# Last six down rows of tokens 0 to 255 with tokens on partitions, and their closing LayerNorm along the free axis

## The chip, the cores and the metric

The kernel runs on one core of a Trainium2 chip. The metric is the device time of one launch in microseconds (us), as the median of several runs. Five engines work from queues of their own: TensorE (PE in the profile; PEld is its weight load), VectorE (DVE), ScalarE (ACT), GpSimd (POOL) and SyncE (SP). SP issues most of the DMAs, in order.

## The reference

One inference step of a one-layer decoder trunk over 512 prompt tokens and 8 x 4 sample tokens, 544 in all, with model width 1024: a SwiGLU feed-forward block with post-LayerNorm, a mixing layer (RWKV-7 heads beside a short convolution) with post-LayerNorm, a second SwiGLU block with post-LayerNorm. The change touches the end of the last block alone:

```python
def layer_norm(x, g, b):
    mu = jnp.mean(xf, axis=-1, keepdims=True)
    var = jnp.mean(jnp.square(xf - mu), axis=-1, keepdims=True)
    return (xf - mu) * lax.rsqrt(var + LN_EPS) * g + b

def swiglu(x, wg, wu, wd):
    return (jax.nn.silu(x @ wg) * (x @ wu)) @ wd

x = layer_norm(ALPHA * x + 0.5 * swiglu(x, p["ffn2_wg"], p["ffn2_wu"], p["ffn2_wd"]), p["ln3_g"], p["ln3_b"])
```

The outputs are `x` for prompt and sample tokens and the states of the mixing layer.

## The kernel before

**Layout.** Activations lie with the 1024 features on partitions, as 8 tiles of 128, and the 544 tokens along the free axis. `z` (128 x 8 x 544) is the residual to which products are added. `HALF` splits the tokens: half 0 is 0 to 255, half 1 is 256 to 543 (288 tokens). `xhl` and `hhl` hold the block's input and the hidden rows, each value as a high and a low fp32r part; weights are loaded to a `raw` tile by SP and split into such a pair in an `hl` tile: ACT writes the high part (L134), DVE the low part (L135). A product is three matmuls (high x high, high x low, low x high; L150 to L152). The `raw` tiles form a ring of 5 in this block, the `hl` tiles a ring of 6, and `hb` tiles (`hlb` in the profile) another one.

**The second block, `f2`.** The 22 hidden rows (`DFF` = 22 x 128) come in the chunks of `CHUNKS`. The first four chunks have four rows and go through a scheme with fewer products (`pairs`, `downs`, L547 to L549). The last chunk has six rows, 16 to 21: `pairs(LAST)` makes them, and `down(LAST, d, h)` multiplies them by the down weights for output tile `d` (128 features) and half `h`: 6 rows x 3 matmuls with a 128x128 block of weights as the stationary operand and 256 or 288 tokens moving. L427 adds the sum to `z`, and `add_sum` (L320, L322) keeps a running sum of the tiles for the mean. `f2` is built with `late = 0`: `main` runs the eight `down`s of half 1, and `end` those of half 0.

**The end of the program.** `weave("l3a", ...)` lays the LayerNorm of half 1 (`layer_norm`, L222 to L268) over the `down`s of half 0: each step of the norm names the TensorE time it wants filled, and so much of the other generator is put behind it. Here the sums over features are matmuls by a matrix of 1/1024 (`ones`), so that the mean and the variance stand on all partitions. After this `layer_norm_end` does the same for half 0: mean matmuls (L275, L276, with three matmuls L278 whose result is not used), subtraction (L288), squares (L289), variance matmuls in plain f32 (L291), Ln and Exp for the inverse root (L292, L293), for two column blocks of 128 tokens; then multiplication (L297), scale and shift per feature (L301 on DVE, L303 on ACT), and a store for each two feature tiles (L304). Half 1 is stored at L315.

**What sets the order.** The code is recorded in program order with `weave`; a list scheduler then places each engine's instructions, within the bounds of `issue_after`. Each engine runs its list in order. A tile of a ring is written again only when its readers are done.

Of the kernel before, what the change touches and what calls it, by code (L numbers as in the profile page):

```python
# [12 lines left out]
F32 = mybir.dt.float32  # L13
F32R = mybir.dt.float32r
AF = mybir.ActivationFunctionType
OP = mybir.AluOpType
# [3 lines left out]
P = 128  # L20
D = 1024
KD = D // P
# [3 lines left out]
NSEQ = 8  # L26
TS = 4
T = TP + NSEQ * TS
B11, B21, B22, NT1, NT2, T3, T4 = range(7)
HALF = ((0, 256), (256, 544))  # L30
# [5 lines left out]
CHUNKS = ((0, 4), (4, 8), (8, 12), (12, 16), (16, 22))  # L36
LAST = len(CHUNKS) - 1
# [21 lines left out]


@with_exitstack
def body(ctx: ExitStack, tc: tile.TileContext, xT, gu1, wd1, win, wo_c, wo_0, wo_1, gu2, wd2, lora, vec, cst,
         sst, cstate, s0, y_o, wkvp_o, wkvs_o, shift_o, conv_o):
    nc = tc.nc
    PE, ACT, DVE, POOL = nc.tensor, nc.scalar, nc.vector, nc.gpsimd
    dma = nc.sync.dma_start

    def pool(st, name, side="left", **kw):
        return st.enter_context(tc.tile_pool(name=name, bufs=1, side=side, reuse_waits="tile", **kw))

    keep = pool(ctx, "keep")
    wp = pool(ctx, "wp")
# [14 lines left out]
    def col(v, i):  # L87
        return vc[:, v + i:v + i + 1]
# [4 lines left out]
    def sm():  # L93
        return ps.tile([P, 512], F32, name="sm", bufs=5)
# [105 lines left out]
    def weave(key, crit, *fill):  # L200
        bg.extend(fill)
        for need in crit:
            take(need * FILL[key])

    def drain(*fill):
        bg.extend(fill)
        take(1e9)
# [5 lines left out]
    def layer_norm(z, c0, c1, gcol, bcol, epsv, q, rs, s1, sink, table=None, hl2=None, both=False):  # L213
        n = c1 - c0
        pair = hl2 is None

        def mean_of(x, need):
            split(hl2[:, 0, :n], hl2[:, 1, :n], x)
            o = sm()
            yield need  # L220
            for i in range(2):
                PE.matmul(o[:, :n], onr, hl2[:, i, :n], start=(i == 0), stop=(i == 1))  # L222
            return o

        if pair:
            m = sm()
            PE.matmul(m[:, :n], ones, s1[:, :n], start=True, stop=False)
            PE.matmul(m[:, :n], ones, z[:, KD - 1, c0:c1], start=False, stop=True)
        else:
            m = yield from mean_of(s1[:, :n], 1300)  # L230
        yield 800 if pair else 300
        for j in range(4):
            zz = z[:, 2 * j:2 * j + 2, c0:c1]
            qq = q[:, 2 * j:2 * j + 2, :n]
            DVE.tensor_tensor(zz, zz, m[:, None, :n].to_broadcast([P, 2, n]), op=OP.subtract)
            sq = ACT.activation(qq, zz, AF.Square)
            if j == 0 and table == "ahead":
                tab = issue(sq, ACT.preload_act_table_set, "natural_log_exp_and_others")
            if pair:
                if j % 2:  # L240
                    DVE.tensor_tensor(q[:, 2 * j - 2:2 * j, :n], q[:, 2 * j - 2:2 * j, :n], qq, op=OP.add)
            elif j:
                DVE.tensor_tensor(q[:, 0:2, :n], q[:, 0:2, :n], qq, op=OP.add)
            yield 900 if pair else 1000
        if pair:
            v = sm()
            for i, j in enumerate((0, 1, 4, 5)):
                PE.matmul(v[:, :n], ones, q[:, j, :n], start=(i == 0), stop=(i == 3))
        else:
            DVE.tensor_tensor(q[:, 0, :n], q[:, 0, :n], q[:, 1, :n], op=OP.add)  # L250
            v = yield from mean_of(q[:, 0, :n], 900)
        yield 800 if pair else 600
        if table == "late":
            tab = issue(ACT.activation(warm, v[:, 0:1], AF.Copy), ACT.preload_act_table_set, "natural_log_exp_and_others")
        ln = ACT.activation(rs[:, :n], v[:, :n], AF.Ln, bias=epsv)
        if table:
            after(ln, tab)
        ACT.activation(rs[:, :n], rs[:, :n], AF.Exp, scale=-0.5)
        yield 1200 if pair else 600
        for d in range(0, KD, 2):  # L260
            zz = z[:, d:d + 2, c0:c1]
            DVE.tensor_tensor(zz, zz, rs[:, None, :n].to_broadcast([P, 2, n]), op=OP.mult)
            for e in (d, d + 1):
                x, g, b = z[:, e, c0:c1], col(gcol, e), col(bcol, e)
                if both and e > d:
                    DVE.tensor_scalar(x, x, g, b, op0=OP.mult, op1=OP.add)
                else:
                    ACT.activation(x, x, AF.Identity, scale=g, bias=b)  # L268
            sink(d, zz, c0, c1)
            yield 1600 if pair else 1700  # L270

    def layer_norm_end(z, gcol, bcol, epsv, q, rs, s1):

        m, o = sm(), sm()
        PE.matmul(m[:, :256], ones, s1[:, :256], start=True, stop=False)  # L275
        PE.matmul(m[:, :256], ones, z[:, KD - 1, 0:256], start=False, stop=True)  # L276
        for _ in range(3):
            PE.matmul(o[:, :256], ones, s1[:, :256], start=True, stop=True)  # L278
        cs = [slice(0, P), slice(P, 2 * P)]

        def two(x):
            return x[:, None, :].to_broadcast([P, 2, P])

        for c in cs:
            v = sm()
            for j in range(0, KD, 2):
                zz, qq = z[:, j:j + 2, c], q[:, j:j + 2, c]
                DVE.tensor_tensor(zz, zz, two(m[:, c]), op=OP.subtract)  # L288
                ACT.activation(qq, zz, AF.Square)  # L289
                for i in range(2):  # L290
                    PE.matmul(v[:, :P], ones, qq[:, i, :], start=(j + i == 0), stop=(j + i == KD - 1))  # L291
            ACT.activation(rs[:, c], v[:, :P], AF.Ln, bias=epsv)  # L292
            ACT.activation(rs[:, c], rs[:, c], AF.Exp, scale=-0.5)  # L293
        for n, c in enumerate(cs):
            for d in range(0, KD, 2):
                zz = z[:, d:d + 2, c]
                DVE.tensor_tensor(zz, zz, two(rs[:, c]), op=OP.mult)  # L297
                for e in (d, d + 1):
                    x, g, b = z[:, e, c], col(gcol, e), col(bcol, e)
                    if e % 2 or e == 6:  # L300
                        DVE.tensor_scalar(x, x, g, b, op0=OP.mult, op1=OP.add)  # L301
                    else:
                        ACT.activation(x, x, AF.Identity, scale=g, bias=b)  # L303
                dma(y_o[:, d:d + 2, c], zz)  # L304
        yield 0

    def to_x(spill):
        def sink(d, x, c0, c1):
# [3 lines left out]
        return sink  # L312

    def to_y(d, x, c0, c1):
        dma(y_o[:, d:d + 2, c0:c1], x)  # L315

    def add_sum(s1, z, d, c0, c1, top):
        n = c1 - c0
# [5 lines left out]
    class Ffn:  # L324
# [21 lines left out]

        def open_lnq(self):
            self.tst.close()
            return pool(self.tst, "lnq" + self.ph).tile([P, KD, 288], F32, name="lnq")

        def weights(self, key, src, n, pair=False):
            if key not in self.w:
# [313 lines left out]
        def main(self):  # L666
            self.open_tv()
            tv = self.inputs()
            self.raw, self.held, self.t = {}, [], 0
            self.todo, self.events = self.plan()  # L670
            z = self.z
            self.done, self.made = set(), set()
            for i, m in enumerate((3, 0, 1, 2) if self.nf > NEX else range(self.na)):
                if m >= self.nf:
                    yield from self.up(m, 0)
                yield from self.up(m, 1)
                next(tv)
                if i == 1 and self.nf < self.na:
                    for j, n in enumerate("gu"):
                        self.w[n, 3] = wload(self.gu[3, :, j, :])  # L680
                elif i in (1, 2):
                    self.t = (-12, -5)[i - 1]
                    self.feed()
            self.t = 0
            for _ in tv:
                pass
            for d in range(KD):
                ACT.activation(z[:, d], z[:, d], AF.Copy, scale=2.0 * ALPHA)
            for ci in range(LAST + 1):
                if ci:  # L690
                    yield from self.pairs(ci)
                if ci < LAST:
                    yield from self.downs(ci)
            for d in range(KD):
                yield from self.down(LAST, d, 1 - self.late)

        def end(self):
            return seq(*(self.down(LAST, d, self.late) for d in range(KD)))
# [773 lines left out]
    weave("l2b", ln2b, f2.first())  # L1472
    drain(f2.main())
    lnq = f2.open_lnq()
    weave("l3a", layer_norm(z, *HALF[1], V_LN3G, V_LN3B, epsf, lnq, f2.lnr, f2.s1[1], to_y, "ahead", f2.hl2), f2.end())
    drain()
    drain(layer_norm_end(z, V_LN3G, V_LN3B, epsf, lnq, f2.lnr, f2.s1[0]))
    f2.close()


# [3 lines left out]
def _constants():  # L1484
# [15 lines left out]
    return c  # L1500


_OUTS = [("y", (P, KD, T)), ("wkvp", (P, 4, 64)), ("wkvs", (P, 4, NSEQ, 64)), ("shift", (P, 14, 9)),
         ("conv", (P, 4, 2 + 2 * NSEQ))]


# [52 lines left out]
```

## Time and profile before

| | |
|---|---|
| median of 3 runs | 1095.28 us (1092.99 to 1095.94) |
| the profiled execution | 1092.91 us |
| its span in the profile | 1091.1 us |
| granted TensorE clock, mean over the span | 0.995 |
| PE / DVE / ACT / POOL busy | 1059.4 / 845.7 / 588.3 / 178.4 us |

Times in the profile run from the start of the span. A row of the timeline has its start, its duration, engine, line, operation, and output and inputs by the program's names; in brackets stands the idle time ahead of it and what ended it. A row of a group has the total busy time and the mean of one instruction in ns. Matmuls overlap, so the distance between two starts is what one costs, not its duration. In the windows each engine has its busy time in the stretch. In the chain of waits a row has its start and the time that it adds.

### The profile page before, as it was taken

To read this page: it belongs to the slowest core of one execution; us is meant where nothing else is said; L and a number is where in the kernel's file an instruction comes from. 1 tells how busy PE (TensorE), PEld (TensorE's weight loads), DVE (VectorE), ACT (ScalarE), POOL (GpSimd) and SP (SyncE) were. 2 spreads that over 40 slices of the span, in tenths; PEclk is the share of its full clock that TensorE was granted. 3 is DMA by queue.
4 is the path that set the end of the run, shared out by engine and by line. 5 is a ranking of instruction groups with operands and counts; after the bars stand their busy time and mean duration, and the time that the engine had idled before them with its cause. 6 is when DMAs were issued, how large, how long until landed. Compare 5 with 4: busy or idle time off the path is not lost.

```text
span 1091.1 us, 22869 instructions
## 1 busy us (share of the span) xinstructions
PE 1059.4 (97%) x9258; PEld 1019.9 (93%) x9258; DVE 845.7 (78%) x1576; ACT 588.3 (54%) x1095; POOL 178.4 (16%) x288
## 2 busy tenths in 40 slices
PE   9999999999999998999999999999999999999997
PEld 8999999999999987898889987999999999999996
DVE  7788988889775857775578558999889888887657
ACT  6645465554552767653435334667555555545425
POOL 0122220313100022142000200001312213121000
PEclk9999999999999999999999999999999999999999
DMA  8568594967853323252145625443857859677402
GB/s 281 135 128 190 119 221 122 184 151 154 193 135 117 97 95 88 63 117 70 41 140 183 145 79 174 120 135 79 180 153 154 196 117 212 153 159 172 122 1 82
DMA packets 99082, 148.88 MB, mean 136 GB/s; under 512 B 35233, under 2 KB 60577, under 8 KB 98977
## 3 DMA queue, kind: packets, MB, share of 16 engines
q1 hardware_dynamic: 71776, 111.25, 33.2%
q0 software_dynamic: 27200, 36.18, 22.0%
q8 instruction: 72, 1.18, 0.4%
q14 instruction: 34, 0.27, 0.1%
HBM read 128.74 MB, written 9.75 MB: 127 GB/s over the span
## 4 chain that ended last, share of the span: by engine, by line
PE 68%; DVE 9%; issue 9%; ACT 7%; DMA 6%; POOL 1%; SPq 0%; POOLq 0%; DVEq 0%; ACTq 0%
PE mm L547 7%; PE mm L150 7%; PE mm L548 7%; PE mm L549 7%; PE mm L151 7%; PE mm L152 7%; PE sm L549 5%; PE sm L548 5%; PE sm L547 5%; DMA raw<-in_gu 4%; ACT hl L134 3%; DVE hl L135 2%; PE sm L1042 1%; PE sm L150 1%; PE sm L151 1%
## 5 line engine op out<-in xcount | busy, mean ns | idle before, releaser
L135 DVE TENSOR_TENSOR hl<-raw,hl 128x1024 fp32r<-128x1024 f32 (+3 forms) x232 | 270.5, 1171 | 75.2 <-ACT hl L134 74.2
L134 ACT ACTIVATE hl<-raw 128x1024 fp32r<-128x1024 f32 (+3 forms) x232 | 231.8, 1013 | 88.8 <-DVE raw L514 40.5
L150 PE MATMUL mm<-xhl,hl 128*128 128x288 f32 (+1 forms) x736 | 219.7, 299 | 3.2 <-DVE z L1431 1.6
L151 PE MATMUL mm<-xhl,hl 128*128 128x288 f32 (+1 forms) x736 | 214.1, 291 | 0.3 <-DVE xhl L139 0.3
L152 PE MATMUL mm<-xhl,hl 128*128 128x288 f32 (+1 forms) x736 | 212.6, 289 | 0.1
L150 PEld LDWEIGHTS mm<-xhl,hl 128*128 128x128 f32 x736 | 139.1, 189 | 10.3 <-DVE z L1431 2.6
L151 PEld LDWEIGHTS mm<-xhl,hl 128*128 128x128 f32 x736 | 139.4, 189 | 2.6 <-issue 1.2
L152 PEld LDWEIGHTS mm<-xhl,hl 128*128 128x128 f32 x736 | 139.2, 189 | 1.2 <-DVE hl L135 0.5
L549 PE MATMUL sm<-xhl,hl 128*128 128x272 f32 x432 | 125.3, 290 | 0.0
L548 PE MATMUL sm<-xhl,hl 128*128 128x272 f32 x432 | 124.5, 288 | 0.0
L547 PE MATMUL sm<-xhl,hl 128*128 128x272 f32 x432 | 124.0, 287 | 0.0
L547 PE MATMUL mm<-tv,hl 128*128 128x272 f32 x288 | 83.2, 289 | 3.4 <-ACT cpb L608 3.1
L520 POOL DMA_DIRECT2D raw<-in_gu x36 | 43.4, 1206 | 256.9 <-DVE hlb L139 155.3
L549 PE MATMUL mm<-tv,hl 128*128 128x272 f32 x288 | 83.4, 290 | 0.0
L548 PE MATMUL mm<-tv,hl 128*128 128x272 f32 x288 | 83.1, 289 | 0.0
L547 PEld LDWEIGHTS sm<-xhl,hl 128*128 128x128 f32 x432 | 81.4, 188 | 0.0
L549 PEld LDWEIGHTS sm<-xhl,hl 128*128 128x128 f32 x432 | 81.3, 188 | 0.0
L548 PEld LDWEIGHTS sm<-xhl,hl 128*128 128x128 f32 x432 | 81.2, 188 | 0.0
L526 POOL DMA_DIRECT2D raw<-in_wd x32 | 39.3, 1482 | 248.8 <-DVE hlb L139 218.0
L547 PEld LDWEIGHTS mm<-tv,hl 128*128 128x128 f32 x288 | 54.3, 188 | 4.7 <-ACT cpb L608 4.7
L547 PE MATMUL mm<-hhl,hl 128*128 128x272 f32 x192 | 56.9, 302 | 0.7 <-DVE z L637 0.7
L547 PE MATMUL sm<-hhl,hl 128*128 128x272 f32 x192 | 55.9, 291 | 0.0
(393 smaller groups left out, 2784.0 us busy)
## 6 DMA issues: line engine op xcount, KB each, us to landing
raw<-in_gu SPq DMA_DIRECT2D x84, 512.0 KB, 4.7
raw<-in_gu POOLq DMA_DIRECT2D x36, 512.0 KB, 6.3
raw<-in_wd SPq DMA_DIRECT2D x32, 512.0 KB, 4.7
raw<-in_win SPq DMA_DIRECT2D x26, 512.0 KB, 3.6
raw<-in_wd POOLq DMA_DIRECT2D x32, 256.0 KB, 6.9
raw<-in_wd SPq DMA_DIRECT2D x16, 384.0 KB, 3.2
z<-cpb POOLq DMA_DIRECT2D x16, 272.0 KB, 9.7
z<-sv POOLq DMA_DIRECT2D x16, 272.0 KB, 6.5
```

The source lines that it names most:

```text
L134: ACT.activation(hl[:, 0, a:b], raw[:, a:b], AF.Copy)
L135: DVE.tensor_tensor(hl[:, 1, a:b], raw[:, a:b], hl[:, 0, a:b].bitcast(F32), op=OP.subtract)
L150: PE.matmul(out, wh, src[:, 0, k, c0:c1], start=(start and i == 0), stop=False)
L151: PE.matmul(out, wh, src[:, 1, k, c0:c1], start=False, stop=False)
L152: seen["fill"] = PE.matmul(out, wl, src[:, 0, k, c0:c1], start=False, stop=(stop and i == n - 1))
L520: POOL.dma_start(x.rearrange("p (s c) -> p s c", s=2), bass.AP(tensor=a11.tensor, offset=a11.offset, ap=[[2 * D, P], [P * 2 * D, 2], [1, 5 ...
L526: POOL.dma_start(four(x)[:, i], bass.AP(tensor=a11.tensor, offset=a11.offset, ap=[[DFF, P], [P * DFF, 2], [1, 256]]), accum_op=OP.add)
L547: PE.matmul(out, wh, src(0, i), start=(first and i == 0), stop=False, skip_group_check=True)
L548: PE.matmul(out, wh, src(1, i), start=False, stop=False, skip_group_check=True)
L549: PE.matmul(out, wl, src(0, i), start=False, stop=(i == n - 1), skip_group_check=True)
L1042: crit(PE.matmul(q[r0:r0 + m, o:o + nn], lhs, rhs, start=True, stop=True))
```

## The change

In `f2`, the `down`s of the last chunk are replaced for both halves.

- Half 1 (`down_wide`, in `main`): the down weights are read as six row tiles of 128 x 1024 (`wl`, one for each hidden row, all features) in place of eight tiles of 128 x 768 (one for each output tile, all six rows). Output tiles 0 to 3 are summed in four PSUM tiles row by row; then tiles 4 to 7 follow one after the other. The six split tiles are kept.
- Half 0 (`end_wide`, laid under half 1's norm): tokens stand on partitions, in two blocks of 128. Eight transposes (a matmul in transpose mode against an identity that is loaded, `eye`) put the residual `z` of the block into two PSUM tiles of 512 features; onto these the products are added, with the hidden rows (128 x 128 tokens) as the stationary operand and 512 columns of the weights moving (the last 512 features of the second block in two parts of 256).
- The norm of half 0 (`layer_norm_rows`): `bn_stats` on four parts of 256 features straight from PSUM, `bn_aggr` for mean and variance of each token, Ln and Exp on one column, and two `scalar_tensor_tensor` for each 512 features: (x - mean) * g, then * rs + b, with `g` and `b` loaded to all partitions (`gb`, 1 MB). The rows go to a new output `yt`, tokens on partitions, with 2 KB for each partition and store. `layer_norm_end` is gone; `add_sum` for half 0 too.

```diff
+    def layer_norm_rows(o, y, g, b, epsv, st, out):
+
+        for i in range(4):
+            DVE.bn_stats(st[:, 6 * i:6 * i + 6], o[i // 2][:, 256 * (i % 2):256 * (i % 2) + 256])
+        mean, rs = st[:, 24:25], st[:, 26:27]
+        DVE.bn_aggr(st[:, 24:26], st[:, 0:24])
+        ACT.activation(rs, st[:, 25:26], AF.Ln, bias=epsv)
+        ACT.activation(rs, rs, AF.Exp, scale=-0.5)
+        for i in range(2):
+            c = slice(512 * i, 512 * i + 512)
+            DVE.scalar_tensor_tensor(y[:, c], o[i], mean, g[:, c], op0=OP.subtract, op1=OP.mult)
+            DVE.scalar_tensor_tensor(y[:, c], y[:, c], rs, b[:, c], op0=OP.mult, op1=OP.add)
+            dma(out[:, c], y[:, c])
...
-        dma(y_o[:, d:d + 2, c0:c1], x)
+        dma(y_o[:, d:d + 2], x)
...
-            for d in range(KD):
-                yield from self.down(LAST, d, 1 - self.late)
+            if self.late:
+                for d in range(KD):
+                    yield from self.down(LAST, d, 0)
+            else:
+                yield from self.down_wide()
+
+        def down_wide(self):
...
+            def weights(m):
+                with ExitStack() as st:
+                    for e in self.held if m > 3 else ():
+                        st.enter_context(tc.issue_after(e.ins))
+                    return wload(wl[m])
+
+            self.wm = []
+
+            def done(d, o):
+                DVE.tensor_tensor(z[:, d, c0:c1], z[:, d, c0:c1], o[:, :n], op=OP.add)
+                add_sum(self.s1[1], z, d, c0, c1, KD)
+
+            def three(o, m, d, first, last):
+                hl, x = self.wm[m], self.hhl
+                for i, (v, y) in enumerate(((0, 0), (0, 1), (1, 0))):
+                    seen["fill"] = PE.matmul(o[:, :n], hl[:, v, P * d:P * d + P], x[:, y, m, c0:c1], start=(first and i == 0),
+                                             stop=(last and i == 2), skip_group_check=True)
+
+            os = [f() for f in (big, sm, big, sm)]
+            for m in range(n6):
+                self.wm.append(weights(m))
+                for d in range(4):
+                    three(os[d], m, d, m == 0, m == n6 - 1)
+                    if d % 2:
+                        yield 6 * (n / 2.4 + 3)
+            for d in range(4):
+                done(d, os[d])
+            for d in range(4, KD):
+                o = big() if d % 2 else sm()
+                for m in range(n6):
+                    three(o, m, d, m == 0, m == n6 - 1)
+                    if m % 2:
+                        yield 6 * (n / 2.4 + 3)
+                done(d, o)
+
+        def end_wide(self, gb, idt, st):
+            n6 = len(self.wm)
+            z, x = self.z, self.hhl
+            for t in range(2):
+                tok = slice(P * t, P * t + P)
+                o = [(sm if t else big)() for _ in range(2)]
+                for d in range(KD):
+                    PE.matmul(o[d // 4][:, P * (d % 4):P * (d % 4) + P], z[:, d, tok], idt, start=(d % 4 == 0), stop=False,
+                              is_transpose=True, skip_group_check=True)
+                yield 1500
+                for c, n in ((0, 512), (512, 256), (768, 256)) if t else ((0, 512), (512, 512)):
+                    q = o[c // 512][:, c % 512:c % 512 + n]
+                    for m in range(n6):
+                        for i, (v, y) in enumerate(((0, 0), (0, 1), (1, 0))):
+                            seen["fill"] = PE.matmul(q, x[:, y, m, tok], self.wm[m][:, v, c:c + n], start=False,
+                                                     stop=(m == n6 - 1 and i == 2), skip_group_check=True)
+                        if m % 2 or n == 512:
+                            yield 3 * n / 2.4 * (1 if n == 512 else 2)
+                layer_norm_rows(o, self.rows[t].rearrange("p a t -> p (a t)")[:, 0:D], gb[:, 0], gb[:, 1], epsf, st[:, t],
+                                yt_o[:, t])
...
-    weave("l3a", layer_norm(z, *HALF[1], V_LN3G, V_LN3B, epsf, lnq, f2.lnr, f2.s1[1], to_y, "ahead", f2.hl2), f2.end())
+    gb = f2.lp.tile([P, 2, D], F32, name="gb")
+    idt = f2.lp.tile([P, P], F32, name="idt")
+    st = f2.lp.tile([P, 2, 28], F32, name="st")
+    dma(idt, eye)
+    dma(gb, bass.AP(tensor=ln3.tensor, offset=ln3.offset, ap=[[0, P], [D, 2], [1, D]]))
+    weave("l3a", layer_norm(z, *HALF[1], V_LN3G, V_LN3B, epsf, lnq, f2.lnr, f2.s1[1], to_y, "ahead", f2.hl2),
+          f2.end_wide(gb, idt, st))
     drain()
-    drain(layer_norm_end(z, V_LN3G, V_LN3B, epsf, lnq, f2.lnr, f2.s1[0]))
     f2.close()
```

The line numbers of the changed kernel differ. In it L696 is the addition to `z` in half 1, L702 a matmul of `down_wide`, L729 a transpose, L736 a matmul of `end_wide`, L275 to L283 the instructions of `layer_norm_rows`; `layer_norm`'s own lines up to L268 have kept their numbers. On TensorE's list, the end of the program before: the last three products, then the statistics of half 0.

```order
L150 MATMUL sm<-hhl,hlb 128x256
L151 MATMUL sm<-hhl,hlb 128x256
L152 MATMUL sm<-hhl,hlb 128x256
L275 MATMUL sm<-cpb,ones 128x256
L278 MATMUL sm<-cpb,ones 128x256
L276 MATMUL sm<-z,ones 128x256
L278 MATMUL sm<-cpb,ones 128x256 x2
L291 MATMUL sm<-lnq,ones 128x128 x16
```

And now, from the last product of half 1 on (the four L222 are the mean and the variance of half 1's norm):

```order
L702 MATMUL mm<-hhl,hl 128x288 x18
L729 MATMUL mm<-idt,z 128x128 x8
L736 MATMUL mm<-hl,hhl 128x512 x3
L222 MATMUL sm<-hhl,ones 128x288
L736 MATMUL mm<-hl,hhl 128x512
L222 MATMUL sm<-hhl,ones 128x288
L736 MATMUL mm<-hl,hhl 128x512 x32
L222 MATMUL sm<-hhl,ones 128x288
L729 MATMUL sm<-idt,z 128x128 x2
L222 MATMUL sm<-hhl,ones 128x288
L729 MATMUL sm<-idt,z 128x128 x6
L736 MATMUL sm<-hl,hhl 128x512 x18
```

Behind these stand 36 more L736 with 256 columns, and nothing after them: the matmuls of half 0's norm are gone, and half 1's variance (the third L222) stands behind all products of the first token block.

VectorE's list at the end, before (L427 and L322 are the addition to `z` and the running sum, L288 to L301 half 0's norm):

```order
L427 TENSOR_TENSOR z<-z,mm 128x256
L322 TENSOR_TENSOR cpb<-cpb,z 128x256
L427 TENSOR_TENSOR z<-z,sm 128x256
L288 TENSOR_TENSOR z<-z,sm 128x2x128 x8
L297 TENSOR_TENSOR z<-z,cpb 128x2x128 x2
L301 TENSOR_SCALAR z<-z,vc 128x128 x2
L297 TENSOR_TENSOR z<-z,cpb 128x2x128 x2
L301 TENSOR_SCALAR z<-z,vc 128x128 x3
```

And now, from half 1's sums of squares (L243, L250) on; `st<-mm` and `hk` belong to the first token block, `st<-sm` and `sv` to the second, and L262 is half 1's multiplication by the inverse root:

```order
L243 TENSOR_TENSOR lnq<-lnq 128x576 x2
L250 TENSOR_TENSOR lnq<-lnq 128x288
L139 TENSOR_TENSOR hhl<-lnq,hhl 128x288
L275 BN_STATS st<-mm 128x6 x2
L277 BN_AGGR st<-st 128x2
L282 SCALAR_TENSOR_TENSOR hk<-mm,st,gb 128x512 x2
L283 SCALAR_TENSOR_TENSOR hk<-hk,st,gb 128x512 x2
L262 TENSOR_TENSOR z<-z,cpb 128x2x288 x4
L275 BN_STATS st<-sm 128x6 x4
L277 BN_AGGR st<-st 128x2
L282 SCALAR_TENSOR_TENSOR sv<-sm,st,gb 128x512 x2
L283 SCALAR_TENSOR_TENSOR sv<-sv,st,gb 128x512 x2
```

The first block's whole norm has moved ahead of half 1's L262; behind the last matmuls only the second block's is left. On SP's list the loads of `eye` and `gb` follow the last weights, and the stores of the first block stand ahead of half 1's four.

More of the change, by code (lines that the diff above doesn't have):

```diff
@@ L61, in body @@
 @with_exitstack
-def body(ctx: ExitStack, tc: tile.TileContext, xT, gu1, wd1, win, wo_c, wo_0, wo_1, gu2, wd2, lora, vec, cst,
-         sst, cstate, s0, y_o, wkvp_o, wkvs_o, shift_o, conv_o):
+def body(ctx: ExitStack, tc: tile.TileContext, xT, gu1, wd1, win, wo_c, wo_0, wo_1, gu2, wd2, wl, ln3, eye, lora, vec, cst,
+         sst, cstate, s0, y_o, yt_o, wkvp_o, wkvs_o, shift_o, conv_o):
     nc = tc.nc
@@ L270, in layer_norm @@
             yield 1600 if pair else 1700
[L272 to L305, printed above, removed]
+    def layer_norm_rows(o, y, g, b, epsv, st, out):
[10 more added lines that the diff above has]
+            dma(out[:, c], y[:, c])
     def to_x(spill):
@@ L348, in open_lnq @@
             self.tst.close()
-            return pool(self.tst, "lnq" + self.ph).tile([P, KD, 288], F32, name="lnq")
+            self.lp = pool(self.tst, "lnq" + self.ph)
+            return self.lp.tile([P, KD, 288], F32, name="lnq")
         def weights(self, key, src, n, pair=False):
@@ L693, in main @@
                     yield from self.downs(ci)
-            for d in range(KD):
-                yield from self.down(LAST, d, 1 - self.late)
+            if self.late:
[4 more added lines that the diff above has]
+        def down_wide(self):
+            m0, m1 = CHUNKS[LAST]
+            n6 = m1 - m0
+            c0, c1 = HALF[1]
+            n = c1 - c0
+            z = self.z
+            def weights(m):
[28 more added lines that the diff above has]
+                done(d, o)
@@ L1500, in _constants @@
     return c
-_OUTS = [("y", (P, KD, T)), ("wkvp", (P, 4, 64)), ("wkvs", (P, 4, NSEQ, 64)), ("shift", (P, 14, 9)),
+_OUTS = [("y", (P, KD, 288)), ("yt", (P, 2, D)), ("wkvp", (P, 4, 64)), ("wkvs", (P, 4, NSEQ, 64)), ("shift", (P, 14, 9)),
          ("conv", (P, 4, 2 + 2 * NSEQ))]
@@ L1529 @@
         a[name] = wo[:, :, k0:k1].reshape(KD // n, n, P, (k1 - k0) * P).transpose(0, 2, 1, 3).reshape(KD // n, P, D)
+    a["wl"] = g["ffn2_wd"][0][CHUNKS[LAST][0] * P:].reshape(-1, P, D)
+    a["ln3"] = np.stack([g["ln3_g"][0], g["ln3_b"][0]])
+    a["eye"] = np.eye(P, dtype=np.float32)
     a["lora"] = np.stack([np.concatenate([g["w_lora_up"][0], g["a_lora_up"][0]], 0), g["g_lora_up"][0]], 1)
@@ L1549 @@
     r = _run(nc, [arrays], core_ids=[0]).results[0]
-    y, wp, ws, sh, cv = (r["out_" + n] for n, _ in _OUTS)
-    y = y.transpose(2, 1, 0).reshape(T, D)
+    y, yt, wp, ws, sh, cv = (r["out_" + n] for n, _ in _OUTS)
+    y = np.concatenate([yt.transpose(1, 0, 2).reshape(2 * P, D), y.transpose(2, 1, 0).reshape(288, D)], 0)
     sh = sh.transpose(2, 1, 0).reshape(9, 14 * P)
```

## The prediction, made before the changed kernel ran

> **What bounds the kernel now.** I read the page first: the totals, then the chain that ended last.
>
> ```profile
> span 1091.1 us, 22869 instructions
> ...
> PE 1059.4 (97%) x9258; PEld 1019.9 (93%) x9258; DVE 845.7 (78%) x1576; ACT 588.3 (54%) x1095; POOL 178.4 (16%) x288
> ...
> PE 68%; DVE 9%; issue 9%; ACT 7%; DMA 6%; POOL 1%; SPq 0%; POOLq 0%; DVEq 0%; ACTq 0%
> ```
>
> TensorE sets the pace, so over most of the program only fewer or cheaper matmuls help. The instruction orders of the two programs are the same up to the last feed-forward chunk, so I cut the trace into the windows that the change touches: the last matmuls of half 0 (tokens 0 to 255), the closing LayerNorm, and what follows the last computation.
>
> ```profile
> core 0: us, PE busy (x) PEld busy (x) DVE busy (x) ACT busy (x) POOL busy (x), PEclk, DMA share, GB/s
> 1059.50:1077.40 17.90, 17.90 (x150) 17.56 (x149) 14.41 (x29) 9.90 (x17) 0.00 (x0) 1.00 0.14 48
> 1077.40:1088.20 10.80, 6.40 (x44) 5.47 (x42) 8.50 (x27) 6.44 (x18) 0.00 (x0) 0.92 0.33 97
> 1088.20:1091.10 2.90, 0.00 (x0) 0.00 (x0) 0.00 (x0) 0.00 (x0) 0.00 (x0) 0.50 0.42 117
> ```
>
> In the first window TensorE never rests. In the second it is idle for a third, and its 44 records belong to the norm alone. The chain of waits over that stretch shows engines handing over to one another:
>
> ```profile
> 1077.43 0.12 PE sm L152
> 1077.55 0.43 PE sm L275 x2
> 1077.98 0.43 PE sm L278 x2
> 1078.42 0.45 PE sm L276 x2
> ...
> 1079.81 2.06 PE sm L291 x16
> ...
> 1081.96 0.37 ACT cpb L292
> 1082.33 0.30 ACT lnq L289
> ...
> 1082.86 0.76 DVE z L297 x2
> ...
> 1087.94 0.26 DVE z L301
> ```
>
> From 1077.55 to 1082.86 statistics are made: 1.3 us for the mean, 1.0 for the first subtraction and square, 2.1 for the variance matmuls, 0.9 for Ln and Exp. From there to 1088.20 VectorE scales and shifts. The last matmul of the real work is 13.5 us ahead of the end of the span: this tail is what the change rewrites.
>
> **The matmuls.** Before, half 0 takes 144 matmuls of 256 columns (8 output tiles, 6 row tiles, 3 terms).
>
> ```profile
> 1059.35 0.28 PE L150 MATMUL mm<-hhl,hl 128*128 128x256 f32 x1
> ...
> 1073.11 0.28 PE L150 MATMUL mm<-hhl,hlb 128*128 128x256 f32 x1
> ...
> 1077.03 0.28 PE L150 MATMUL sm<-hhl,hlb 128*128 128x256 f32 x1
> ...
> 1077.27 0.28 PE L152 MATMUL sm<-hhl,hlb 128*128 128x256 f32 x1
> ...
> 537.56 1.02 PE L1207 MATMUL sm<-ux,BS 128*128 128x512 f32 x2
> ...
> L1207 PE MATMUL sm<-ux,BS x8: 590/592/697, 537.6 to 662.5; 128*128 128x512 f32 x8
> ...
> 433.28 0.52 PE L951 MATMUL sm<-cs,bkb 64*128 64x64 f32 x10
> ...
> L951 PE MATMUL sm<-cs,bkb 64*128 64x64 f32 x64 | 4.2, 236 | 1.4 <-ACT BK L956 1.0 <-DVE SC L940 0.3
> ```
>
> Between the second and third row lie 33 matmuls: 3.92/33 = 0.1188 us each, 17.1 for 144. From 1059.35 to 1077.39 are 18.0, so the four ones-matmuls (L222) of half 1's norm take 0.9 with their waits; they stay. The new code has 54 matmuls of 512 columns and 36 of 256. No fp32r matmul of 512 columns is in the trace. Twice the 256 row is 0.238. The plain f32 matmul of L1207 has 512 columns in two records, 1.02 less one record of 0.59, 0.43, apart, and plain f32 passes of 256 columns (L275, above) are 0.43/2 = 0.215 apart, 1.81 times the fp32r row, which puts 512 at 0.43/1.81 = 0.238 too; half of 0.43, with no overhead per instruction, is 0.215. I take 0.226, between them: 54 x 0.226 + 36 x 0.1188 = 16.5 us, 0.6 less than before; 15.9 and 17.1 at the ends.
>
> The residual now needs 16 transposes of 128x128 f32. The nearest row is L951, f32 transposes of 64x64 (236 ns busy), ten in 0.52 us: (0.52 - 0.24)/9 = 0.03 us apart, though there two row halves of the array alternate. The other side is a 128-column plain f32 matmul, two records of L291, 2.06/16 x 2 = 0.26. A transpose is one record in the trace, not two, but each loads its own 128 columns of weights, as each 256-column matmul does in 0.119. I take 0.12: 1.9 us, with 0.5 and 4.1 at the ends.
>
> The Trainium skill, "TensorE: Matmul & The Clock Gate", Part 4 (PE-mode transpose), speaks against this: it gives about 275 ns for a 128x128 bf16 transpose inside a kernel, mostly latency. If that were the spacing, 16 would take an estimated 4.4 us, and the sum below would lose 2.5 us. The L951 rows speak for a duration: 236 ns busy but 0.03 apart.
>
> TensorE then issues its last matmul's end at 1059.35 + 1.9 + 16.5 + 1.0 (L222 and 0.1 more of waiting, since fewer matmuls stand ahead of the first one) = 1078.75.
>
> **What leaves the critical path.** Mean and variance matmuls, squares, the eight subtractions and the scale and shift per column (L275 to L304) are gone; so are eight z additions and six running sums of half 0 on VectorE. For tokens 0 to 127 the new norm runs under the matmuls of tokens 128 to 255; only the second half's tail is exposed.
>
> ```profile
> 1077.59 0.42 DVE L427 TENSOR_TENSOR z<-z,sm 128x256 f32<-128x256 f32 x1 [1.26 <-PE sm L152]
> ...
> L288 DVE TENSOR_TENSOR z<-z,sm 128x256 f32<-128x256 f32 x8 | 2.7, 416 | 0.9 <-PE sm L276 0.9
> ...
> L1256 DVE SCALAR_TENSOR_TENSOR zc<-cu,vc,zc 128x512 f32<-128x512 f32 x8 | 6.0, 746 | 0.7 <-ACT zc L1254 0.7
> L1003 DVE TENSOR_TENSOR tm<-AT,De 128x15 f32<-128x15 f32 x4 | 0.7, 172 | 0.1
> L713 ACT ACTIVATE warm<-eps 128x1 f32<-128x1 f32 x1 | 0.2, 203 | 0.0
> out_y<-z SPq DMA_DIRECT2D x4, 288.0 KB, 2.3
> out_y<-z SPq DMA_DIRECT2D x8, 128.0 KB, 1.9
> ```
>
> VectorE starts 0.32 after a last matmul's start (1077.27 to 1077.59), so at 1078.63 + 0.32 = 1078.95. No bn_stats is in the trace; as a one-pass read of 256 PSUM columns it is nearest to L288, 0.42 (0.17 if it cost as little as the smallest row, 0.84 if it made two passes). Only the fourth is exposed: the others wait for column blocks done 4.3 and 2.1 us earlier. bn_aggr on 24 numbers: 0.17, from L1003. So statistics end at 1079.54. Ln and Exp on one column are 0.2 each (L713), to 1080.0, hidden by the first two scalar_tensor_tensor, which need only the mean. Four of those on 512 columns: 0.746 each, about 0.67 apart when chained (other chained VectorE rows overlap by 0.08: eight L288 of 0.416 in 2.74), 2.76 in all, to 1082.3 (0.3 less by a two-operand row, 0.2 more unchained). Then a store: before, from 1088.20 to 1091.10 are 2.9 with 128 KB; the stores are now 256 KB, and the 288 KB row lands 0.4 later: 3.3 (up to 0.5 more, as two follow each other). End of span: 1085.6.
>
> **What is hidden, and by what.** The half-1 sums are now made row tile by row tile, over four output tiles at once.
>
> ```profile
> 1040.41 0.29 PE L549 MATMUL sm<-xhl,hl 128*128 128x272 f32 x1
> ...
> 1042.72 0.73 DVE L139 TENSOR_TENSOR hhl<-sv,hhl 128x544 fp32r<-128x544 f32 x1
> ...
> 1065.47 0.76 DVE L243 TENSOR_TENSOR lnq<-lnq 128x576 f32<-128x576 f32 x1
> ...
> 1071.70 0.76 DVE L262 TENSOR_TENSOR z<-z,cpb 128x576 f32<-128x576 f32 x1
> 1072.50 4.26 ACT L268 ACTIVATE z<-z,vc 128x288 f32<-128x288 f32 x8 [0.83 <-DVE z L262]
> ...
> L135 DVE TENSOR_TENSOR hl<-raw,hl 128x1024 fp32r<-128x1024 f32 (+3 forms) x232 | 270.5, 1171 | 75.2 <-ACT hl L134 74.2
> ...
> 1040.00:1050.00 10.00, 10.00 (x76) 9.85 (x75) 7.92 (x16) 1.86 (x3) 0.00 (x0) 1.00 0.00 0
> ```
>
> A weight tile is used up in 12 matmuls, 1.6 us, where an output tile lasted 18. The first four tiles' weights are split before the last pair product is issued, by 1040.54. From there 140 matmuls fill the time to 1059.35, 0.134 each; row tile 4 is 44 of them, 5.9 us, away, at 1046.4, while its rows were ready at 1043.45 before, and the two weight splits left, now 1.17 instead of 0.95 each, end near 1045. Cover is over 1 us; without it a late split costs up to 1.2. The 64 KB identity and the 1 MB of scale and shift go out on SP's queue behind the last weights, where the 1040 to 1050 window shows no DMA traffic; neither is needed before 1059 and 1069. SP then waits for the first rows' result before half 1's stores; those follow ACT's L268 anyway.
>
> VectorE works in order: the first row block's statistics (its columns are ready at 1059.35 + 1.0 + 0.5 + 18 x 0.226 = 1064.9 and 18 matmuls later, 1069.0) stand between half 1's sums of squares (1065.47 before) and its L262. Ahead of L262 now stand two bn_stats, bn_aggr and four 512-column operations, 3.7 us, from 1069.1: L262 starts near 1073 rather than 1071.70, and ACT's L268 (4.3 us) ends near 1078, before ACT's next Ln at 1079.5. So this delay stays off the path by 1.5 us.
>
> **The sum.** The span falls from 1091.1 to 1085.6, by 5.5 us. With the 1.8 us that lie around the span the profiled execution, 1092.91, becomes 1087.4. That execution was below all three timed runs; against their median of 1095.28 the prediction is **1089.8**. The unknown prices that help add up to 1.4 + 0.6 + 0.25 + 0.3 + 0.4 (if the stores cost no more) = 3.0, those that hurt to 2.2 + 0.6 + 0.4 + 0.2 + 0.5 = 3.9: gains of 1.6 to 8.5, 1086.8 to 1093.7 for this case.
>
> **Rivals.**
> *Dear transposes.* At 0.26 each, with bn_stats in two passes, the gain is 5.5 - 2.2 - 0.4 = 2.9: 1092.4. For it: no 128x128 transpose is in the trace, and a change between f32 and fp32r may cost TensorE something that no row shows apart. Against: one record per transpose.
> *512-column matmuls at half rate.* If fp32r with 512 moving columns ran like L1207's records, 0.43 apart, 54 x (0.43 - 0.226) = 11.0 us would be added and TensorE, never idle there, would pass it all on: 1100.8, slower. It decides from 0.226 + 5.5/54 = 0.33 us. For it: L1207 is the only 512-column row. Against: its operands are plain f32, whose 256-column records also cost almost twice.
> *VectorE's and ACT's order becomes the bound.* If the first row block's norm came 5 us late, L268 would end at 1083 and hold ACT's last Ln and Exp behind it to 1083.4; the third scalar_tensor_tensor needs them at 1079.54 + 1.34 = 1080.9. The end is 2.5 later, 1092.3. For it: VectorE's queue is in order and 14.41 of 17.9 busy already. Against: it loses fourteen operations of 0.34 there and gains twelve, four of them twice as long.
> That the tail does not shrink at all would need the end to be set elsewhere; half 1's stores, last issued near 1078, land by 1081.
>
> **How the numbers follow.** Forecast 0.70; dear transposes 0.13; half rate 0.10; the order 0.07. What this kernel's measurement can tell from no change is about 0.3%, 3.3 us. The forecast's own range is beyond that for 0.67 of its 0.70; dear transposes straddle it (0.04 faster, 0.09 within), the order too (0.02 and 0.05), half rate is slower. Faster 0.73, within 0.3% 0.17, slower 0.10. The timed runs before scatter by 3 us, so I widen the case's range by 1.5 us on either side, to 1085.3 and 1095.2, which also holds the two middle rivals; half rate stays out.
>
> **What would show it.** After the change: last L736 near 1078.6; 512-column rows 0.22 to 0.24 apart; eight transposes in about 1 us; one bn_stats, bn_aggr and four scalar_tensor_tensor between the last matmul and the last store, 3.7 us; no TensorE gap after 1040 longer than 0.3 us; ACT done with L268 before the last bn_aggr. The prediction is wrong if TensorE's end moves past 1081, if the tail from last matmul to end exceeds 9 us, or if the half-1 rows show TensorE waiting for a weight split.

## The result and the profile after

| | before | after |
|---|---|---|
| median, 6 runs each | 1095.12 us (1092.99 to 1096.86) | 1089.48 us (1087.87 to 1091.27) |
| ratio | | 0.9951 (0.9936 to 0.9966) |
| the profiled execution: span | 1091.12 us | 1088.24 us |
| start of the last six down rows | 1036.75 | 1038.78 |
| from there to the end of the span | 54.37 us | 49.47 us |
| of it: half 1 | 22.60 | 22.38 |
| half 0, first instruction to the end of the last matmul | 18.20 | 19.89 |
| behind the last matmul | 13.57 | 7.20 |

The changed kernel is faster by 0.49% (0.34 to 0.64), 5.6 us between the medians. The two profiled spans lie only 2.9 apart, since this execution came 2.0 us later to the place where the programs part. Ahead of it TensorE and GpSimd have the same instructions; on ACT and VectorE only four splits of down weights differ, which are 1024 columns wide in place of 768, and SP loads those wider tiles. They are not what makes this start late: some 700 us ahead of them, at TensorE's 2500th matmul, the changed kernel is already 2.3 us behind (328.25 against 325.96). The first experiment shows how far the start scatters. What is compared below is the stretch from the first matmul of the last six down rows to the end. The ends of the spans are taken from the trace in full; the page of the profile gives them to 0.1 us, and the expectations below, worked out from it, have 54.35 and 49.42 for 54.37 and 49.47.

The chain of waits of the changed kernel over that end (start, time that the row adds, engine, line); L702 is half 1, L729 the transposes, L736 half 0's products:

```profile
1058.92 2.40 PE mm L702 x18
1061.32 0.87 PE mm L729 x8
1062.20 0.69 PE mm L736 x3
1062.89 0.36 PE sm L222
1063.24 0.23 PE mm L736
1063.48 0.26 PE sm L222
1063.73 7.43 PE mm L736 x32
1071.16 0.31 PE sm L222
1071.47 0.22 PE sm L729 x2
1071.69 0.28 PE sm L222
1071.96 0.65 PE sm L729 x6
1072.62 8.45 PE sm L736 x54
1081.06 0.02 issue
1081.08 0.77 DVE st L275 x2
...
1081.88 0.27 DVE st L277
...
1082.18 0.81 DVE sv L282 x2
```

Up to 1081.06 TensorE alone carries the chain. Behind the last product the chain before changed engines five times and took 10.6 us to the last computation; now VectorE alone stands there, for 3.8 us, and then come the stores. The timeline shows first the weight load of half 1's first mean matmul, then both norms of half 0 on VectorE and ACT (start, busy time, in brackets the idle time ahead and what ended it):

```profile
1062.84 0.19 PEld L222 LDWEIGHTS sm<-hhl,ones 128*128 128x128 f32 x1 [0.38 <-ACT hhl L138]
...
1072.51 1.42 DVE L282 SCALAR_TENSOR_TENSOR hk<-mm,st,gb 128x512 f32<-128x512 f32 x2
...
1073.84 1.41 DVE L283 SCALAR_TENSOR_TENSOR hk<-hk,st,gb 128x512 f32<-128x512 f32 x2
...
1075.16 2.76 DVE L262 TENSOR_TENSOR z<-z,cpb 128x576 f32<-128x576 f32 x4
1075.95 4.27 ACT L268 ACTIVATE z<-z,vc 128x288 f32<-128x288 f32 x8 [2.55 <-DVE z L262]
...
1077.84 0.76 DVE L275 BATCH_NORM_STATS2 st<-sm 128x6 f32<-128x256 f32 x2
1081.08 0.76 DVE L275 BATCH_NORM_STATS2 st<-sm 128x6 f32<-128x256 f32 x2 [2.49 <-PE sm L736]
1081.88 0.26 DVE L277 BATCH_NORM_AGGREGATE st<-st 128x2 f32<-128x24 f32 x1
1082.18 0.29 ACT L278 ACTIVATE st<-st,eps 128x1 f32<-128x1 f32 x1 [1.96 <-DVE st L277]
1082.18 1.41 DVE L282 SCALAR_TENSOR_TENSOR sv<-sm,st,gb 128x512 f32<-128x512 f32 x2
1082.50 0.20 ACT L279 ACTIVATE st<-st 128x1 f32<-128x1 f32 x1
1083.50 1.40 DVE L283 SCALAR_TENSOR_TENSOR sv<-sv,st,gb 128x512 f32<-128x512 f32 x2
```

The first block's norm (`hk`) runs while TensorE makes the second block's products. Of the second block's four bn_stats two start at 1077.84, and two, not one, wait 2.49 us for TensorE's last matmul. Ln and Exp end at 1082.70 beside the first two operations of 512 columns. VectorE ends at 1084.90; the last 3.3 us hold the two stores, which land 2.0 us after their issue, and the 1.3 us from there to the end of the program.

### The profile page after: what moved, and what is told of

It reads as the page before. It is cut to its first block, busy times and chain, and to the rows that moved or that the text cites. A ratio compares the mean times of both kernels' runs of the same rounds, so it can differ in the third digit from the quotient of the medians.

```text
span 1088.2 us, 22658 instructions
## 1 busy us (share of the span) xinstructions
PE 1054.5 (97%) x9178; PEld 1013.2 (93%) x9178; DVE 841.3 (77%) x1550; ACT 583.1 (54%) x1077; POOL 179.5 (16%) x288
## 4 chain that ended last, share of the span: by engine, by line
PE 69%; DVE 9%; issue 8%; ACT 6%; DMA 5%; POOL 1%; SPq 0%; DVEq 0%; POOLq 0%; ACTq 0%
PE mm L527 8%; PE mm L528 7%; PE mm L529 7%; PE mm L150 7%; PE mm L151 6%; PE mm L152 6%; PE sm L529 5%; PE sm L527 5%; PE sm L528 5%; DMA z<-cpb 2%; ACT hl L134 2%; DVE hl L135 2%; DMA raw<-in_gu 1%; PE sm L1088 1%; PE mm L702 1%
```

## The experiments

All compare the stretch defined above. Its parts are read from the timeline: the first matmul of the last six down rows, the first instruction of half 0, the end of the last product's matmul, the end of the span.

| kernel | start | end | stretch | half 1 | half 0 | behind it | time of its own run or runs |
|---|---|---|---|---|---|---|---|
| before | 1036.75 | 1091.12 | 54.37 | 22.60 | 18.20 | 13.57 | 1095.12 |
| e0_before | 1037.33 | 1091.70 | 54.37 | 22.60 | 18.20 | 13.57 | 1093.47 |
| after | 1038.78 | 1088.24 | 49.47 | 22.38 | 19.89 | 7.20 | 1089.48 |
| e1_wide_only | 1038.24 | 1092.52 | 54.27 | 22.39 | 18.19 | 13.69 | 1094.28 |
| e2_no_residual | 1035.93 | 1083.37 | 47.44 | 22.39 | 17.86 | 7.20 | 1085.14 |
| e3_norms_last | 1036.28 | 1090.40 | 54.12 | 22.39 | 20.14 | 11.59 | 1092.16 |
| e4_256 | 1042.66 | 1092.42 | 49.76 | 22.38 | 20.18 | 7.19 | 1094.18 |
| e5_third_tile | 1040.64 | 1089.99 | 49.34 | 22.39 | 19.90 | 7.05 | 1091.78 |
| e6_mean_later | 1040.34 | 1089.41 | 49.08 | 22.39 | 19.48 | 7.21 | 1091.17 |
| e7_both | 1037.76 | 1086.70 | 48.94 | 22.39 | 19.48 | 7.07 | 1087.53 |

Where a kernel ran once, its time says little: it moves with the start, by nearly 7 us between kernels that are the same up to there, while the stretch of one and the same kernel came out as 54.37 twice. Times of different jobs do not compare either: the kernel before has a median of 1095.12 in the first job and of 1092.49 (11 runs) in the one that ran e4 to e7.

**The kernel before once more** (`e0_before`, no edit).

> The kernel before, unchanged, profiled once more. The quantity that these experiments compare is the stretch from the first matmul of the last six down rows to the end of the span: 54.35 us before (1036.75 to 1091.1), 49.42 after the change (1038.78 to 1088.2). Theory (the 2.0 us by which the changed kernel reaches this stretch later is scatter of the 1037 us ahead of it, which hold the same instructions in the same order): the stretch is again 54.2 to 54.5, and the place where it starts may move by 1 to 2 us. Rival (the change itself delays what runs ahead, by where its inputs lie): the start is again 1036.5 to 1037.0 here, and near 1038.8 in every kernel with the new inputs.

The stretch is 54.37. The start moved by 0.6 here; with the new inputs it lies at 1035.93 and 1036.28 (e2, e3) as well as at 1038.78 and 1042.66. The rival falls: its 1038.8 does not recur, and the spread has no side. Why these starts scatter was not tried. The granted clock may have a part in it: the two latest starts, e4 and e5, have the lowest means over the span, 0.991 and 0.992. It is not all, since e3 starts early with 0.993 and the kernel after late with 0.995.

**The row tiles alone** (`e1_wide_only`): half 1 as in the change, half 0 from the same tiles with features on partitions, then the old norm.

```diff
-    weave("l3a", layer_norm(...), f2.end_wide(gb, idt, st))
+    weave("l3a", layer_norm(...), f2.end_rows())
     drain()
+    drain(layer_norm_end(z, V_LN3G, V_LN3B, epsf, lnq, f2.lnr, f2.s1[0]))
...
+        def end_rows(self):
+            for d in range(KD):
...
+                    for i, (v, y) in enumerate(((0, 0), (0, 1), (1, 0))):
+                        PE.matmul(o[:, :n], self.wm[m][:, v, P * d:P * d + P], self.hhl[:, y, m, c0:c1], ...)
```

> Half 1 by down_wide with the six row tiles of weights as in the change; half 0 from the same tiles but with features on partitions, 144 matmuls of 256 columns, and the old norm at the end. Theory (the row tiles cost nothing and gain nothing, all of the gain is in half 0's products and tail): stretch 54.0 to 54.6. Rival (the row tiles themselves save or cost, since TensorE no longer waits for weights or now does): stretch off 54.35 by more than 0.5.

The stretch is 54.27. Half 1 is 0.2 shorter, here as in every kernel with row tiles, and the rest is as before within 0.1; its chain has the old statistics again (L289 to L307 are the lines of the old norm here):

```profile
1076.68 2.14 PE mm L785 x18
1078.82 0.43 PE sm L289 x2
...
1081.08 2.07 PE sm L305 x16
...
1084.13 0.76 DVE z L311 x2
...
1089.21 0.26 DVE z L315
```

So nearly all of the gain comes with half 0's part of the change, its products and norm together. The row tiles, which those products read, cost nothing. They save 0.2, which the kernel before spends at 1042.74: there a weight load waits for ACT's split of the last two hidden rows (L138, 1042.03 to 1042.69), which the order by row tiles needs later.

**Without the transposes** (`e2_no_residual`).

```diff
-                for d in range(KD):
-                    PE.matmul(o[d // 4][...], z[:, d, tok], idt, start=(d % 4 == 0), stop=False, is_transpose=True, ...)
-                yield 1500
...
-   PE.matmul(q, x[:, y, m, tok], self.wm[m][:, v, c:c + n], start=False, ...)
+   PE.matmul(q, x[:, y, m, tok], self.wm[m][:, v, c:c + n], start=(m == 0 and i == 0 and c % 512 == 0), ...)
```

> The change without the 16 transposes: half 0's outputs leave out the residual. Theory (transposes are on TensorE's path at about 0.11 us each, and fewer instructions ahead of half 1's mean make it wait up to 0.5 more): stretch 1.2 to 1.8 shorter than 49.42, so 47.6 to 48.2. Rival (a transpose is latency, hidden under the next matmuls, or the change of mode costs more than the rows show): less than 0.8, or more than 2.3.

The stretch is 47.44, 2.03 shorter, all of it in half 0: a little more than expected. The transposes are on TensorE's path at their full distance, 1.74 us by the chain above (0.87 for eight, twice). Leaving them out saves some 0.3 us more, because the scheduler then finds another order: between the two L222 of a pair stand two and three products, in place of one product and two transposes, and the four L222 cost 0.86 in all, where they cost 1.21 after the change. That they would wait longer was wrong.

```profile
1060.11 0.28 PE sm L222
...
1060.85 0.13 PE sm L222
...
1068.17 0.32 PE sm L222
...
1069.20 0.13 PE sm L222
```

Neither rival holds.

**Both norms behind the last matmul** (`e3_norms_last`): the second block's first, then the first block's.

```diff
-                layer_norm_rows(o, self.rows[t]...)
+                os.append(o)
...
+            last = rows(1)
+            with tc.issue_after(last.ins):
+                rows(0)
```

> The change with the first token block's norm put behind the second's on VectorE, so that both stand behind the last matmul. Theory (the tail is VectorE's work behind the last matmul plus one store, so what is hidden now comes out in full: four bn_stats, bn_aggr and four operations of 512 columns, 1.4 + 0.3 + 2.7): stretch 4.2 to 4.6 longer than 49.42, 53.6 to 54.0, and the gain is nearly gone. Rival (the gain is in the cheaper norm, not in hiding half of it; the two blocks' work overlaps with the store): 1 to 2.5 longer.

The stretch is 54.12, 4.65 longer, 0.1 above the range, and 4.39 of it lie behind the last matmul; the rest is in half 0's matmul part, where TensorE now waits 0.16 for half 1's variance. VectorE's timeline shows the first block's work (`mm`, `hk`) standing there in full:

```profile
1078.85 0.76 DVE L275 BATCH_NORM_STATS2 st<-sm 128x6 f32<-128x256 f32 x2 [3.53 <-PE sm L737]
...
1081.27 1.41 DVE L283 SCALAR_TENSOR_TENSOR sv<-sv,st,gb 128x512 f32<-128x512 f32 x2
1082.59 1.42 DVE L275 BATCH_NORM_STATS2 st<-mm 128x6 f32<-128x256 f32 x4
1084.04 0.26 DVE L277 BATCH_NORM_AGGREGATE st<-st 128x2 f32<-128x24 f32 x1
1084.34 1.41 DVE L282 SCALAR_TENSOR_TENSOR hk<-mm,st,gb 128x512 f32<-128x512 f32 x2
1085.67 1.41 DVE L283 SCALAR_TENSOR_TENSOR hk<-hk,st,gb 128x512 f32<-128x512 f32 x2
```

With both blocks exposed the whole change is worth 0.25 us against the kernel before, and 0.2 of this is half 1's: the tail is 2.0 shorter (13.57 to 11.59), and half 0's matmul part 1.9 longer (18.20 to 20.14). What carries the gain is that half of the new norm is hidden. The old form, with features on partitions, cut into the same two token blocks and hidden in the same way, was not run; so it is not shown that hiding needs tokens on partitions.

**Products of 256 columns** (`e4_256`).

```diff
-                for c, n in ((0, 512), (512, 256), (768, 256)) if t else ((0, 512), (512, 512)):
+                for c, n in ((0, 256), (256, 256), (512, 256), (768, 256)):
```

> The change with all products of half 0 in matmuls of 256 columns, 144 in place of 54 of 512 and 36 of 256. Theory (an fp32r matmul costs its columns plus a small fixed amount, 0.232 for 512 against 0.119 for 256): 54 x (2 x 0.119 - 0.232) = 0.3 us longer, stretch 49.5 to 49.9. Rival (512 columns ran at a worse rate than the rows show, part of a waiting TensorE): 0.5 or more shorter.

The stretch is 49.76, 0.29 longer, as the theory had it. The second block's 72 products are 0.119 apart, so two matmuls of 256 columns take 0.238 where one of 512 takes 0.232: the wider one runs at the same rate and saves a small fixed part.

```profile
1076.66 8.58 PE sm L736 x72
```

**A third PSUM tile** (`e5_third_tile`) for the last 256 features, with normalisation and store in pieces of 512, 256 and 256.

```diff
-                o = [(sm if t else big)() for _ in range(2)]
+                o = [sm(), sm(), big()] if t else [big(), big()]
...
-        for i in range(2):
-            c = slice(512 * i, 512 * i + 512)
+        for i, (a, n) in enumerate(((0, 512), (512, 256), (768, 256)) if len(o) > 2 else ((0, 512), (512, 512))):
+            c = slice(a, a + n)
```

> The change with the last 256 features of the second token block in a PSUM tile of their own, and the last store in two of 128 KB. Theory (the third bn_stats stood behind the last matmul only because it shared that matmul's tile): one bn_stats less behind the last matmul, 0.34, one fixed part of two more operations, 0.16, and a last store half as large, 0.2 to 0.4 sooner: stretch 48.8 to 49.1, and the third bn_stats over 1 us ahead of the last matmul's end. Rival (it waited for VectorE's own queue or for the matmuls in front): the third bn_stats again behind the last matmul, stretch 49.3 to 49.6.

```profile
1079.68 0.76 DVE L275 BATCH_NORM_STATS2 st<-sm 128x6 f32<-128x256 f32 x2
1080.84 0.43 DVE L275 BATCH_NORM_STATS2 st<-sm 128x6 f32<-128x256 f32 x1 [0.39 <-PE sm L738]
1082.97 0.43 DVE L275 BATCH_NORM_STATS2 st<-mm 128x6 f32<-128x256 f32 x1 [1.70 <-PE mm L738]
...
1083.73 1.14 DVE L283 SCALAR_TENSOR_TENSOR sv<-sm,st,gb 128x512 f32<-128x512 f32 x2
...
1086.36 0.48 DVE L284 SCALAR_TENSOR_TENSOR sv<-sv,st,gb 128x256 f32<-128x256 f32 x1
```

The mechanism is as stated: the third bn_stats starts at 1080.84, 2.1 us ahead of the fourth, which alone waits for the last matmul. But the stretch is 49.34, a miss: only 0.13 is left, and the number lies in the rival's range. The statistics end 0.33 sooner behind the last matmul. Six operations in place of four take 3.11 us (1083.73 to 1086.84) against 2.72, where 0.16 more was expected, and from VectorE's end to the end of the span it is 0.20 less: -0.33 + 0.39 - 0.20 = -0.14, behind the last matmul.

**The mean later** (`e6_mean_later`): for half 1's norm at the end only.

```diff
-            for i in range(2):
-                PE.matmul(o[:, :n], onr, hl2[:, i, :n], start=(i == 0), stop=(i == 1))
+            for i in range(2):
+                with ExitStack() as es:
+                    if sink is to_y:
+                        es.enter_context(tc.issue_after(seen["fill"].ins))
+                    PE.matmul(o[:, :n], onr, hl2[:, i, :n], start=(i == 0), stop=(i == 1))
+                if i == 0 and sink is to_y:
+                    yield 700
...
-            m = yield from mean_of(s1[:, :n], 1300)
+            m = yield from mean_of(s1[:, :n], 3000 if sink is to_y else 1300)
```

> The change with the four matmuls of half 1's mean and variance (L222) placed further back in TensorE's order, behind six products in place of three for the mean. Theory (TensorE waits for the split sum, 0.4 to 0.9 us in all, as fewer instructions stood ahead of it): stretch 0.4 to 0.9 shorter, 48.5 to 49.0. Rival (the idle time is the price of changing between f32 and fp32r operands, not a wait): unchanged within 0.2.

The stretch is 49.08, 0.39 shorter, just short of the range, and all of it in half 0's matmul part (19.48 against 19.89). The chain of this kernel (L225 is the mean and variance matmul, L741 a product, L734 a transpose), and behind it one row of ACT's timeline:

```profile
1063.76 1.39 PE mm L741 x6
1065.15 0.13 PE sm L225
1065.28 0.69 PE mm L741 x3
1065.97 0.13 PE sm L225
1066.11 6.26 PE mm L741 x27
1072.37 0.87 PE sm L734 x8
1073.24 0.38 PE sm L225
...
1072.72 0.44 ACT L138 ACTIVATE hhl<-lnq 128x288 fp32r<-128x288 f32 x1 [1.96 <-DVE lnq L255]
```

The two mean matmuls cost 0.13 each in place of 0.36 and 0.26: those were waits. The first variance matmul, behind the transposes, still costs 0.38, and this too is a wait: ACT's split of the sum runs from 1072.72 to 1073.16 in this kernel, and the matmul starts at 1073.22. The rival falls.

**Both edits** (`e7_both`).

> Third PSUM tile and later mean together. Theory: the two gains add, stretch 48.0 to 48.7, and the time 6.0 to 6.8 us below the kernel before, where the change itself was 5 to 5.6 below. Rival (what TensorE saves is waited for elsewhere): stretch within 0.3 of the better of the two alone.

The stretch is 48.94, 0.53 below the change, which is what the two gains add to (0.13 + 0.39). It is above the theory's range, since e5's part was mis-sized, and 0.14 below e6 alone, so that the rival's number fits too; but its reason does not, since nothing of either gain is lost. The median is 5.0 us below that of the kernel before in the same job, short of the range as well. In time it has 0.9950 (0.9932 to 0.9968) of the kernel before, against 0.9951 of the change in its own job: the runs cannot tell the two apart.

## Why the prediction was right, point by point

- **The time.** 1089.8 was forecast, 1089.48 measured. The range held it, and the direction and size are the forecast's own case; none of the rivals came about. That the two times agree to 0.3 us is luck: 5.5 us less were forecast, the stretch gave 4.9, and medians of one kernel in two jobs lie 2.6 apart.
- **The matmuls.** Forecast 0.226 for 512 columns, measured 7.43/32 = 0.232; that is 0.3 us in all. Half rate falls with this row and with e4.
- **The transposes.** Forecast 0.12 each, between 0.03 and 0.26; measured 0.87/8 = 0.109. The row that came nearest was the 256-column matmul, which also loads 128 columns of weights each time. The lower end, 0.03, counts matmuls of two row halves that run side by side; within one half the L951 are 0.06 apart. The 275 ns that the Trainium skill gives in "TensorE: Matmul & The Clock Gate", Part 4 (PE-mode transpose), for a bf16 transpose agree with the 272 ns that each of these f32 transposes is busy here, but not with their distance: a sum with that as the distance has 4.4 us for the sixteen, an estimate, where 1.74 were measured.
- **Waits of half 1's mean.** Forecast 1.0 us for the four L222, measured 0.36 + 0.26 + 0.31 + 0.28 = 1.21. "No TensorE gap after 1040 longer than 0.3" was slightly off: the weight load of the first L222 waits 0.38 for ACT (first row of the timeline above). With six products ahead of it, in e6, this wait is gone.
- **What is exposed behind the last matmul.** Forecast 6.7 us, measured 7.20. The term that failed is "only the fourth is exposed": the third bn_stats waits too (+0.34), because it reads the tile that the last matmuls still write, as e5 shows by giving it a tile of its own. bn_stats was sized right (0.42 to 0.43); bn_aggr was taken from a row that was too cheap (0.17, measured 0.26). The four operations (2.72 against 2.76) and the stores (3.3) came as stated.
- **TensorE's end.** The prediction named an end past 1081 as a sign of being wrong, and by the letter it came: the last matmul ends at 1081.05. But 2.03 of it is the later start. From the start of the stretch it is 42.27 us, where the forecast's last matmul, 1078.63 and 0.28 for its duration, lies 42.16 behind the start before.
- **The order on VectorE and ACT.** L262 started at 1075.16 and L268 ended at 1080.22, both about 2 us later than forecast, as was everything; L268 was clear 2.0 us before the last Ln, where 1.5 were forecast. That rival would have needed a delay of 4 to 5 us.
- **The weight splits.** Half 1 takes 22.38 us against 22.60. The one wait of TensorE's weight loads in it, 0.19 at 1039.43, is for ACT's L597 and stands in the kernel before as well (1037.40): TensorE waits for no weight.
- **The sum.** The stretch shortened by 4.9 us where 5.5 were forecast. The difference is 0.2 gained in half 1, 0.3 lost in half 0's part (0.3 in the products and 0.2 in the waits, less 0.2 in the transposes) and 0.5 lost behind the last matmul. The medians differ by 5.6, but with an interval of 3.7 to 7.0 that is no closer a test than the stretch.

## What to carry to other kernels

A norm that follows the last product can be cut into token blocks, so that one block's norm runs under the next block's products; here that cover is worth 4.4 us, while the new form of the norm by itself, 2.0 shorter, pays just for the 1.9 by which half 0's matmul part grows, transposes above all. Before a piece is called hidden because its columns are done early, ask which tile it reads: a tile that is still written makes it wait to the end. And small pieces behind the last matmul cost a fixed part each, which can eat what the earlier start gives.

## What was not expected of the hardware

- The transposes: 272 ns busy each, but 0.109 us apart, f32 of 128x128 one after the other.
- A 256 KB store with 2 KB per partition lands in 2.0 to 2.1 us, where 288 KB in pieces of 1152 bytes took 2.3 and 128 KB in pieces of 512 bytes 1.9: between these, the size hardly matters to the last store.
- The place where the last stretch begins moved between 1035.93 and 1042.66 us over ten executions with the same matmuls ahead of it, while the stretch itself came out as 54.37 us in both executions of the kernel before; half 1's part was 22.38 or 22.39 in all eight kernels with row tiles.
